# Retention with its tiles in three pools, sums of squares for two heads at a time, and two subtractions on VectorE instead of GpSimd

## The chip, the cores and the metric

The kernel runs on one NeuronCore of a Trainium2 chip. Five engines work side by side, each through its own instruction queue in order: TensorE (PE in the profile; its weight loads are listed as PEld), VectorE (DVE), ScalarE (ACT), GpSimd (POOL) and SyncE (SP). SP computes nothing; it issues nearly all of this kernel's DMAs. ACT issues the loads of the projections' weights. PE, DVE and ACT reach both on-chip memories, the large SBUF and the small PSUM into which PE writes; here POOL is used on SBUF tiles only.

The metric is the device time of one execution in microseconds (us). The kernel before took 1909.71 us, the median of three runs (1906.38, 1909.71 and 1910.21).

## What is computed

One layer of a streaming encoder on a sequence of 2048 frames with 1024 channels. A projection of the normalised input gives the operands of two branches. Branch A is chunked attention with 8 heads. Branch B, the one that matters here, is retention with 8 heads, 64 key channels and 128 value channels each. Both are gated, projected, merged, projected again, added to the input and normalised. Cut to what the change touches (`qc` is scaled, `intra_decay`, `cross_decay`, `state_decay` and `chunk_decay` are powers of the head's decay):

```python
s = einsum('bnqhd,bnkhd->bnhqk', qc, kc) * intra_decay        # scores, masked by decay
o_intra = einsum('bnhqk,bnkhe->bnqhe', s, vc)
kv = einsum('bnkhd,hk,bnkhe->nbhde', kc, state_decay, vc)
state = state * chunk_decay + kv                               # from chunk to chunk
o_cross = einsum('bnqhd,nbhde->bnqhe', qc, state_prev) * cross_decay
o = o_intra + o_cross
var = mean(square(o - mean(o)))                                # per frame and head, over 128 channels
o = (o - mean(o)) * rsqrt(var + GN_EPS) * gn_gain
```

The kernel centres the values `v` beforehand, so that the mean of `o` is zero and the variance is a plain sum of squares divided by 128.

## The kernel before

All products are made in the type fp32r, and every operand is split in two for accuracy: an upper part, which is a copy to fp32r made by ACT, and a lower part, which is the operand minus its upper part. A product is then three matmuls (upper by upper, upper by lower, lower by upper).

The program goes through these stages: projections of queries, keys and values of the first half of the sequence (`p0`), attention and retention of the first half, the same for the second half (`p1`, `heads(1)`), then the two output projections of the branches (`ba`, `br`) and the last one (`out`). The gate projections (`g0`, `g1`) have no stage of their own. They are a stream of dense matmul steps, and attention and retention call `fill(n)` to put n steps of this stream between their own matmuls. A step of the gate stream is a group of three matmuls of 512 columns. `later(n, fn)` puts work on the other engines n steps after the present one, and `put(n, dst, src)` does so for a store that SP issues. The order in which each engine gets its instructions is fixed by these calls: `keep_in_program_order` holds for all engines up to the last stages.

Retention (`retention`, L1612) treats two heads at a time (pair `p`, 0 to 3) and a stretch `st` of 256 frames. A pair and a stretch are called a unit here: 16 units in each half, 32 in all; a unit has two items, one for each head `i`. What a unit does:

- SP loads keys and queries for the scores (`load_scored`: tile `ks`, shown as kr, and two tiles `q`, shown as qr, each with two DMAs), and keys and values for the state and the output (`load_valued`: kd and two tiles vr). Each of these six tiles is 128 x 512. Keys and queries are asked for two units ahead, the others one unit ahead. Decay masks (dm, 128 x 384) are loaded once for four units of a pair.
- `scores` (L1668): four matmuls into PSUM tile sr. One step later DVE multiplies by the mask into `sm`, two steps later ACT copies the upper part `sh`, two steps later POOL subtracts into the lower part `sl` (L1692).
- `update` (L1697): the product of keys and values, and the state on DVE.
- `output` (L1742): two matmuls with the state (shown as `o<-qr,sstk`) and six with the parts of the scores. Both heads of a unit write into one PSUM bank, `o`, of which there is one.
- `evacuate` (L1759): once both heads are done, ACT copies `o` to `oz`, squares it to `o2`, and two steps later copies the squares' upper part `o2h`; two further steps later POOL makes the lower part `o2l` (L1783). SP stores `oz` (shown as `ors<-oz`). In the next unit, `sums` adds the squares up over the channels: a matmul with a one-hot column puts each sum into one row of PSUM tile `ssq`. Row `8 * b + 2 * p + i` holds 512 frames of one head, so a unit takes four matmuls of 256 columns, for two heads and two parts.

At the end of a half, `ssq` (32 rows of 512) goes through an inverse square root on DVE to DRAM (`rsscr`). `finish_yr` (L1237) later reads one head's row of 512 into all 128 partitions (tile rb) and scales by it.

All tiles of retention but the state come from one ring, `E` (L114, tag `"e"`), of `E_RET = 22` buffers of 128 x 512 fp32. A new tile takes a buffer whose tile has had its last use, and the instruction that writes it waits until that use is over: the last reader of an operand, or the landing of a store. PSUM accumulators of the gate stream come from a ring of four (`ACC`), and their sums in SBUF from a ring of six (`C`).

Of the kernel before, what the change touches and what calls it, by code (L numbers as in the profile page):

```python
# [11 lines left out]
F32 = mybir.dt.float32  # L12
F32R = mybir.dt.float32r
# [3 lines left out]
ALU = mybir.AluOpType  # L17
# [4 lines left out]
P = 128  # L22
# [6 lines left out]
B = 512  # L29
NB = SEQ // B  # L30
T = 256
# [22 lines left out]
CS = 6  # L54
E_PROJ = 19
E_ATT = 11
E_RET = 22
E_MRG = 23
PR_BUFS = 5
ATT_FILLS = (1.0, 1.0)  # L60
# [9 lines left out]
ONE = 31  # L70
# [3 lines left out]
def hybrid_kernel(  # L74
# [28 lines left out]
    epool, xpool = [None], [None]  # L103

    def r32(ap):
        return ap.bitcast(F32)
# [7 lines left out]
    def E(name, dt=F32, shape=(P, 512)):  # L114
        return epool[0].tile(list(shape), dt, tag="e", name=name)
# [4 lines left out]
    def D(name, shape, dt=F32):  # L120
        return dram.tile(list(shape), dt, name=name)

    def open_phase(name, e_bufs, tr_bufs=0):
        st = ExitStack()
        phase[0] = st
        epool[0] = st.enter_context(tc.tile_pool(name=f"e_{name}", bufs=e_bufs, reuse_waits="tile"))
        if tr_bufs:
            xpool[0] = st.enter_context(
                tc.tile_pool(name=f"tr_{name}", bufs=tr_bufs, space=PSUM, reuse_waits="tile")
            )  # L130
        return st
# [21 lines left out]
    pe, act, dve, pool = Ordered(nc.tensor), Sometimes(nc.scalar), Sometimes(nc.vector), Sometimes(nc.gpsimd)  # L153
    dma = Ordered(nc.sync).dma_start
# [9 lines left out]
    ohr = const.tile([P, NOH], F32R, name="ohr")  # L164
# [28 lines left out]
    rsscr = [D(f"rss_{s}", [32, B]) for s in range(2)]  # L193
# [51 lines left out]
    def later(n, fn):  # L245

        order[0] += 1
        deferred.append((steps[0] + n, order[0], fn, free[0]))
        deferred.sort(key=lambda e: e[:2])
# [8 lines left out]
    def put(lag, dst, src):  # L258

        later(lag, lambda: dma(dst, src))  # L260
# [75 lines left out]
    class Strassen(Chunk):  # L336
        tag = ""
# [899 lines left out]
    def finish_yr(h, b, m, lead, hold=0):  # L1237

        a, u, r = (E(f"{n}_{h}_{b}") for n in ("yr", "yv", "rb"))
        dma(a, orscr[h // 2][b][h % 2])  # L1240
        dma(u, urscr[h][b])
        dma(r, rsscr[b // 2][8 * b + h].rearrange("(o d) -> o d", o=1).broadcast_to([P, B]))

        def gated():
            dve.scalar_tensor_tensor(a, a, gn[:, h:h + 1], u, ALU.mult, ALU.mult)

        later(lead, gated)
        later(lead + 2, lambda: (pool if m is None else dve).tensor_tensor(a, a, r, ALU.mult))
        if m is None:
            put(lead + 8, yrscr[h], a)  # L1250
            return
        wh, wl = (w[:, h % 4, :] for w in R[m])
        at = max(lead + 5, hold - steps[0])
        later(at, lambda: act.copy(wh, a))
        later(at + 2, lambda: dve.tensor_tensor(wl, a, r32(wh), ALU.subtract))
# [356 lines left out]
    def retention(s, ps_ret):  # L1612
        RET_FILL = RET_FILLS[s]
        ssq = ps_ret.tile([32, 512], F32, tag="ssq", bufs=1, name="ssq")
# [3 lines left out]
        tiles, values, dms = {}, {}, {}  # L1618
        begun = [False]
# [36 lines left out]
        def load_state(p, st):  # L1656

            if st == 4:
# [2 lines left out]
                dma(r32(sstk).rearrange("p i c -> p (i c)"), r32(skscr[p]))  # L1661
                sstks[p, 4] = sstk

        def load_mask(p, i):
            dms.setdefault(p, []).append(E(f"dm_{p}_{i}")[:, 0:T + P])
            dma(dms[p][i], dmask[2 * p + i])

        def scores(p, st, i):  # L1668

            nm = f"{p}_{st}_{i}"  # L1670
            ks, qs = tiles[p, st]
            sp = ps_ret.tile([P, 512], F32, tag="sr", bufs=2, name=f"sr_{nm}")[:, 0:T + P]
            for kk in range(2):
                o = sp[:, kk * T:T + kk * P]
                kcol = ks[:, i, kk * P:(kk + 1) * P]
                pe.matmul(o, kcol, qs[i][:, 0, kk * P:], start=True, stop=False)
                pe.matmul(o, kcol, qs[i][:, 1, kk * P:], start=False, stop=True)
            got = []

            def masked():  # L1680
                sm = E(f"sm_{nm}")[:, 0:T + P]
                dve.tensor_tensor(sm, sp, dms[p][i], ALU.mult)
                later(2, lambda: high(sm))

            def high(sm):
                got.append(E(f"sh_{nm}", F32R)[:, 0:T + P])
                act.copy(got[0], sm)
                later(2, lambda: low(sm))

            def low(sm):  # L1690
                got.append(E(f"sl_{nm}", F32R)[:, 0:T + P])
                pool.tensor_tensor(got[1], sm, r32(got[0]), ALU.subtract)  # L1692

            later(1, masked)
            return got
# [41 lines left out]
        def sure(here):  # L1737

            while not here():
                emit()  # L1740
# [18 lines left out]
        def evacuate(p, st, ops):  # L1759
            b, un = st // 2, st % 2  # L1760
            nm = f"{p}_{st}"
            got = []

            def out_():
                oz = E(f"oz_{nm}")
                o2 = E(f"o2_{nm}")
                act.copy(oz, ops)
                act.activation(o2, ops, AF.Square)
                put(
                    2,  # L1770
                    orscr[p][b][:, :, un * T:(un + 1) * T].rearrange("i p t -> p i t"),
                    oz.rearrange("p (i t) -> p i t", i=2),
                )
                later(2, lambda: high(o2))

            def high(o2):
                got.append(E(f"o2h_{nm}", F32R))
                act.copy(got[0], o2)
                later(2, lambda: low(o2))

            def low(o2):
                got.append(E(f"o2l_{nm}", F32R))
                pool.tensor_tensor(got[1], o2, r32(got[0]), ALU.subtract)  # L1783

            later(1, out_)

            def sums():
                sure(lambda: len(got) == 2)
                for i in range(2):
                    r = 8 * b + 2 * p + i  # L1790
                    for n, t in enumerate(got):
                        pe.matmul(
                            ssq[:, un * T:(un + 1) * T], ohr[:, ONE - r:ONE - r + 32],
                            t[:, i * T:(i + 1) * T],
                            start=not begun[0], stop=(p == 3 and st == 4 * s + 3 and i == 1 and n == 1),
                            skip_group_check=True,
                        )
                        begun[0] = True

            return sums  # L1800

        load_scored(*todo[0])
        for i in range(2):
            load_mask(0, i)
# [53 lines left out]
    st = open_phase("proj0", E_PROJ, 4)  # L1858
# [71 lines left out]
    def heads(s):  # L1930

        st = open_phase(f"att{s}", E_ATT)
        with tc.tile_pool(name=f"sbp{s}", bufs=1, reuse_waits="tile") as sbp:
            with tc.tile_pool(name=f"ps_wide{s}", bufs=1, space=PSUM, reuse_waits="tile") as ps_wide:
                attention(s, sbp, ps_wide)
                flush()
        st.close()
        st = open_phase(f"ret{s}", E_RET)
        with tc.tile_pool(name=f"ps_ret{s}", bufs=1, space=PSUM, reuse_waits="tile") as ps_ret:
            retention(s, ps_ret)  # L1940
            flush()
        return st
# [5 lines left out]
    st = heads(0)  # L1948
# [4 lines left out]
    st = open_phase("proj1", E_PROJ, 4)  # L1953
    ch = jobs[2].chunks[1]
    ch.b = {}
    for key in ("b11", "b12", "b21", "b22"):
        ch.b[key] = E(f"{key}_p1", shape=(P, 4, P))
        j, h = int(key[1]) - 1, int(key[2]) - 1
        dma(ch.b[key], w_cols(w_in, jobs[2].cols[1], 2, j)[:, :, h * P:(h + 1) * P])
    run_to(end["g0"])  # L1960
    for h in range(HEADS):
        later(10 + 44 * h, lambda h=h: finish_yr(h, 0, None, 18))
# [4 lines left out]
    st = heads(1)  # L1967
# [4 lines left out]
    st = open_phase("mrg", E_MRG, 4)  # L1972

    free_at = end["br0"] - 12
    for s, (first, every, of) in enumerate((YR_0, YR_1)):
        for n, (i, h) in enumerate((i, h) for i in range(1 - s, 2) for h in range(HEADS)):
            hold = free_at + h % 4 if s and i and h > 3 else 0
            later(
                first + every * n // of,
                lambda s=s, i=i, h=h, hold=hold: finish_yr(h, 2 * s + i, RYR[s][i, h // 4], 8, hold),  # L1980
            )
# [60 lines left out]
```

## Time and profile before

| what | before |
|---|---|
| median of three runs | 1909.71 us |
| profiled execution | 1909.69 us |
| its span in the profile | 1907.9 us |
| mean granted TensorE clock | 0.997 of full speed |
| PE busy | 1866.9 us (98%), 10213 matmuls |
| DVE busy | 1355.7 us (71%) |
| ACT busy | 933.1 us (49%) |
| POOL busy | 665.3 us (35%) |
| retention's masked scores (`sm`), first and last start | 572.2 and 1479.1 us |

Retention takes two stretches of the span, from about 571 to 735 us and from about 1325 to 1497 us. The span is the time from the first to the last instruction of the program in the profile. Busy time is the time in which an engine has an instruction under way; matmuls overlap one another, so a busy PE may still do less than it could. In the views of groups, waits and time below, `sh<-sm` reads "the instruction that writes sh and reads sm". Nearly all instructions carry line 143, since a helper records them, so they are told apart by the tiles. A wait is put down to what came last by the semaphores.

### The profile page before, as it was taken

The page shows a single profiled execution, that of the slowest core. Times are in us where ns is not written, and L with a number is a line of the kernel's source. Part 1 is how long each engine was busy: PE and PEld are TensorE (multiplying, and loading weights), DVE is VectorE, ACT ScalarE, POOL GpSimd, SP SyncE. Part 2 cuts the span into 40 slices and gives each one's busy share as a digit, 9 for nine tenths or more (in the row PEclk, how much of TensorE's full clock was granted, in tenths as well). Part 3 has the DMA queues.
Part 4 walks back from the last instruction along what each step waited for, and adds up shares of the span by engine and source line. Part 5 has one row for each costly group of instructions (what it writes and reads, how often), then busy time and mean ns, then how long its engine had stood idle before and what let it go on. Part 6 is the DMA issues. An engine that isn't in the chain of part 4 may idle for free. (4 is left out here: it accounts for less than half of the span.)

```text
span 1907.9 us, 31062 instructions
## 1 busy us (share of the span) xinstructions
PE 1866.9 (98%) x10213; PEld 1604.4 (84%) x10213; DVE 1355.7 (71%) x2456; ACT 933.1 (49%) x1931; POOL 665.3 (35%) x583
## 2 busy tenths in 40 slices
PE   7999999999999999999999999999999999999998
PEld 6899889888888888899889888887888878888886
DVE  6879888677655658889798677765546766767665
ACT  7555554666654455443333666664455321223544
POOL 0102105455645561001105554554564000002775
PEclk9999999999999999999999999999999999999999
DMA  6586976666549987775776656555998999986673
GB/s 197 158 275 200 282 265 213 185 193 185 175 144 278 279 257 258 231 233 195 222 247 202 185 165 180 166 150 155 275 283 265 326 355 345 322 291 227 209 238 127
DMA packets 325553, 435.88 MB, mean 228 GB/s; under 512 B 29880, under 2 KB 191184, under 8 KB 325392
## 3 DMA queue, kind: packets, MB, share of 16 engines
q1 hardware_dynamic: 260096, 368.35, 60.7%
q10 hardware_dynamic: 65296, 65.55, 11.2%
q8 instruction: 81, 1.33, 0.3%
q14 instruction: 80, 0.66, 0.1%
HBM read 288.14 MB, written 145.64 MB: 227 GB/s over the span
## 5 line engine op out<-in xcount | busy, mean ns | idle before, releaser
L143 POOL TENSOR_SCALAR pr<-pr,rsum 128x640 f32<-128x640 f32 (+4 forms) x128 | 100.0, 781 | 197.7 <-DVE rsum L143 130.7
L143 DVE TENSOR_TENSOR ptl<-tp,pth 128x512 fp32r<-128x512 f32 (+1 forms) x168 | 100.3, 597 | 91.7 <-ACT pth L143 77.8
L143 ACT ACTIVATE pr<-pr,mn 128x640 f32<-128x640 f32 (+4 forms) x128 | 97.9, 765 | 123.3 <-DVE mn L143 97.3
L143 PE MATMUL ps_g_x<-r,wh_g 128*128 128x512 f32 x448 | 141.5, 397 | 1.0 <-ACT u_g L143 0.9
L143 PE MATMUL ps_g_z<-r,wh_g 128*128 128x512 f32 x448 | 141.1, 396 | 0.0
L143 POOL TENSOR_TENSOR l_vr<-vrt,h_vr 128x512 fp32r<-128x512 f32 x32 | 47.7, 1492 | 202.4 <-DMA qrs<-l_q 131.6
L143 POOL TENSOR_TENSOR t_out<-raw_out 128x512 f32<-128x512 f32 x7 | 14.1, 2008 | 263.2 <-DVE wl_out L143 263.2
L143 DVE CUSTOM_DVE_ANT_0 pr<-wide,bt 128x640 f32<-128x640 f32 (+4 forms) x128 | 93.7, 732 | 16.5 <-PE wide L143 13.5
L143 ACT CAST pth<-tp 128x512 fp32r<-128x512 f32 (+1 forms) x168 | 85.3, 507 | 38.9 <-PE tp L143 34.2
L143 PE MATMUL wide<-ka,qa 128*128 128x384 f32 (+1 forms) x448 | 94.9, 327 | 2.9 <-DVE mn L143 2.7
L143 DVE TENSOR_TENSOR sm<-sr,dm 128x384 f32<-128x384 f32 x64 | 35.6, 556 | 85.3 <-PE sr L143 33.9
L143 ACT CAST wh_p<-raw_p 128x512 fp32r<-128x512 f32 x111 | 67.9, 618 | 51.0 <-PE ps_p_y L143 18.2
L143 POOL TENSOR_TENSOR sl<-sm,sh 128x384 fp32r<-128x384 f32 x64 | 69.8, 1090 | 64.8 <-ACT sh L143 44.0
L143 PEld LDWEIGHTS tp<-ident,pr 128*128 128x128 f32 x560 | 71.8, 141 | 23.5 <-POOL pr L143 1.0
L143 PEld LDWEIGHTS ps_g_x<-r,wh_g 128*128 128x128 f32 x448 | 79.6, 189 | 13.9 <-ACT u_g L143 2.3
L143 PEld LDWEIGHTS ps_g_z<-r,wh_g 128*128 128x128 f32 x448 | 79.5, 188 | 12.4
L143 PE MATMUL tp<-ident,pr 128*128 128x128 f32 x560 | 89.0, 272 | 0.3
L143 PE MATMUL ps_g_z<-r,wl_g 128*128 128x512 f32 x224 | 88.2, 394 | 0.0
L143 PE MATMUL ps_g_x<-r,wl_g 128*128 128x512 f32 x224 | 88.1, 393 | 0.0
L143 POOL TENSOR_TENSOR wl_g<-t_g,wh_g 128x512 fp32r<-128x512 f32 x56 | 75.5, 1349 | 35.1 <-ACT wh_g L143 33.8
L143 DVE TENSOR_TENSOR wl_p<-raw_p,wh_p 128x512 fp32r<-128x512 f32 x111 | 79.5, 723 | 7.7 <-ACT wh_p L143 5.4
L143 POOL TENSOR_TENSOR t_g<-raw_g,t_g 128x512 f32<-128x512 f32 x56 | 73.8, 1318 | 28.1 <-issue 8.9
(927 smaller groups left out, 6016.7 us busy)
## 6 DMA issues: line engine op xcount, KB each, us to landing
raw_g<-in_w_in_dram ACTq DMA_DIRECT2D x56, 512.0 KB, 4.9
raw_p<-in_w_in_dram ACTq DMA_DIRECT2D x50, 512.0 KB, 5.8
qa<-qas SPq DMA_DIRECT2D x128, 128.0 KB, 3.4
qr<-qrs SPq DMA_DIRECT2D x128, 128.0 KB, 4.8
vr<-vrs SPq DMA_DIRECT2D x64, 256.0 KB, 5.6
ka<-kas SPq DMA_DIRECT2D x56, 256.0 KB, 4.1
va<-vas SPq DMA_DIRECT2D x40, 256.0 KB, 3.4
kds<-kdt_k SPq DMA_DIRECT2D x32, 256.0 KB, 4.8
```

Of the source, the lines that this page charges most:

```text
L143: return tc.keep_in_program_order(op(*a, **k))
```

## The change

There are four edits.

1. Retention's tiles come from three rings. Loads keep `E`, now with 11 buffers of 128 x 512. Masks and the three tiles of the scores (`sm`, `sh`, `sl`) come from `D_`, 9 buffers of 128 x 384. The four tiles of the output (`oz`, `o2`, `o2h`, `o2l`) come from `O_`, 4 buffers of 128 x 512. In bytes for each partition this is 22,528 + 13,824 + 8,192 = 44,544, where 22 buffers took 45,056.
2. The lower parts `sl` and `o2l` are subtracted on DVE and no longer on POOL.
3. `sums` takes both heads in one matmul of 512 columns: two matmuls for each unit and no longer four. The layout of `ssq` changes with it: row `4 * st + p` holds both heads of a unit, 256 frames each.
4. `finish_yr` reads a head's factors from two rows of this layout, 256 numbers from each, where it read 512 from one.

```diff
-E_RET = 22
+E_RET = 11
+D_RET = 9
+O_RET = 4
...
-        dma(r, rsscr[b // 2][8 * b + h].rearrange("(o d) -> o d", o=1).broadcast_to([P, B]))
+        by_head = rsscr[b // 2].rearrange("(b u p) (i t) -> b p i u t", u=2, p=4, i=2)
+        dma(
+            r.rearrange("p (u t) -> p u t", u=2),
+            by_head[b, h // 2, h % 2].rearrange("(o u) t -> o u t", o=1).broadcast_to([P, 2, T]),
+        )
...
+        def D_(name, dt=F32):
+            return epool[0].tile([P, T + P], dt, tag="d", bufs=D_RET, name=name)
+
+        def O_(name, dt=F32):
+            return epool[0].tile([P, 512], dt, tag="o", bufs=O_RET, name=name)
...
-            dms.setdefault(p, []).append(E(f"dm_{p}_{i}")[:, 0:T + P])
+            dms.setdefault(p, []).append(D_(f"dm_{p}_{i}"))
...
-                sm = E(f"sm_{nm}")[:, 0:T + P]
+                sm = D_(f"sm_{nm}")
...
-                got.append(E(f"sh_{nm}", F32R)[:, 0:T + P])
+                got.append(D_(f"sh_{nm}", F32R))
...
-                got.append(E(f"sl_{nm}", F32R)[:, 0:T + P])
-                pool.tensor_tensor(got[1], sm, r32(got[0]), ALU.subtract)
+                got.append(D_(f"sl_{nm}", F32R))
+                dve.tensor_tensor(got[1], sm, r32(got[0]), ALU.subtract)
...
-                oz = E(f"oz_{nm}")
-                o2 = E(f"o2_{nm}")
+                oz = O_(f"oz_{nm}")
+                o2 = O_(f"o2_{nm}")
...
-                got.append(E(f"o2h_{nm}", F32R))
+                got.append(O_(f"o2h_{nm}", F32R))
...
-                got.append(E(f"o2l_{nm}", F32R))
-                pool.tensor_tensor(got[1], o2, r32(got[0]), ALU.subtract)
+                got.append(O_(f"o2l_{nm}", F32R))
+                dve.tensor_tensor(got[1], o2, r32(got[0]), ALU.subtract)
...
-                for i in range(2):
-                    r = 8 * b + 2 * p + i
-                    for n, t in enumerate(got):
-                        pe.matmul(
-                            ssq[:, un * T:(un + 1) * T], ohr[:, ONE - r:ONE - r + 32],
-                            t[:, i * T:(i + 1) * T],
-                            start=not begun[0], stop=(p == 3 and st == 4 * s + 3 and i == 1 and n == 1),
-                            skip_group_check=True,
-                        )
-                        begun[0] = True
+                r = 4 * st + p
+                for n, t in enumerate(got):
+                    pe.matmul(
+                        ssq, ohr[:, ONE - r:ONE - r + 32], t, start=not begun[0],
+                        stop=(p == 3 and st == 4 * s + 3 and n == 1), skip_group_check=True,
+                    )
+                    begun[0] = True
```

## The prediction, made before the change was run

> **What bounds the kernel now.** I read the busy times first, then a table of stretches: both stretches of retention (571:735 and 1325:1497), one of projection, one of output projection, one with a dip of the clock, one of attention. The columns are busy time and instructions of PE, PEld, DVE, ACT and POOL, the granted clock, the DMA share and GB/s.
>
> ```profile
> span 1907.9 us, 31062 instructions
> PE 1866.9 (98%) x10213; PEld 1604.4 (84%) x10213; DVE 1355.7 (71%) x2456; ACT 933.1 (49%) x1931; POOL 665.3 (35%) x583
> ...
> 571.00:735.00 164.00, 156.80 (x911) 134.79 (x911) 92.54 (x179) 79.25 (x156) 93.09 (x77) 0.99 0.87 257
> 1325.00:1497.00 172.00, 168.40 (x973) 145.14 (x973) 91.33 (x173) 85.58 (x166) 91.58 (x75) 1.00 0.93 280
> 825.00:850.00 25.00, 25.00 (x211) 25.00 (x210) 21.11 (x43) 10.46 (x25) 1.30 (x1) 1.00 0.85 286
> 1575.00:1600.00 25.00, 25.00 (x112) 20.71 (x111) 15.01 (x24) 4.25 (x7) 0.00 (x0) 1.00 0.97 346
> 700.00:725.00 25.00, 22.75 (x128) 19.71 (x127) 12.58 (x22) 9.84 (x21) 14.75 (x13) 0.93 0.55 169
> 1075.00:1100.00 25.00, 24.75 (x144) 21.27 (x143) 16.76 (x39) 16.10 (x37) 15.11 (x15) 1.00 0.55 167
> ```
>
> PE sets the pace: outside retention it has no gap that this change could close. Inside, it is idle for 164.00 - 156.80 = 7.2 us and 172.00 - 168.40 = 3.6 us. This 10.8 us, and what a slower clock costs (0.93 in 700:725), is nearly all that can be won. Who holds PE there is in the waits of PE, first of the first stretch, then of the second (total, times, longest):
>
> ```profile
> PE o L143 <- ACT o L143: 4.2, 4, 2.3
> PE sr L143 <- DMA qr<-qrs: 1.0, 2, 0.6
> PE kv L143 <- DMA vr<-vrs: 0.7, 1, 0.7
> ...
> PE ssq L143 <- POOL o2l L143: 0.5, 1, 0.5
> ```
>
> ```profile
> PE o L143 <- DMA sstk<-sks: 1.4, 1, 1.4
> PE o L143 <- ACT o L143: 1.4, 1, 1.4
> PE o L143 <- POOL sl L143: 0.4, 1, 0.4
> PE ssq L143 <- POOL o2l L143: 0.2, 1, 0.2
> ```
>
> The largest, 4.2 + 1.4 = 5.6 us, is PE waiting for ACT to read the bank `o`. Why ACT is late stands in the group of `sh` and in ACT's timeline; the last row is PE's timeline at the longest of these waits.
>
> ```profile
> L143 ACT CAST sh<-sm 128x384 fp32r<-128x384 f32 x64 | 32.9, 514 | 71.8 <-DMA ors<-oz 49.9 <-DVE sm L143 18.9 <-POOL sl L143 2.2
> ```
>
> ```profile
> 667.88 0.52 ACT L143 CAST sh<-sm 128x384 fp32r<-128x384 f32 x1 [5.57 <-DMA ors<-oz]
> ...
> 669.34 0.57 ACT L143 COPY oz<-o 128x512 f32<-128x512 f32 x1
> 669.82 0.60 ACT L143 ACTIVATE o<-o 128x512 f32<-128x512 f32 x1
> ```
>
> ```profile
> 708.67 0.80 PE L143 MATMUL o<-qr,sstk 128*128 128x256 f32 x2 [2.25 <-ACT o L143]
> ```
>
> `sh` reads nothing of `oz`. It waits because it was given the buffer out of which the store of an earlier `oz` is still being read: 49.9 us in all. ACT is in order, so `oz` and the squaring queue behind `sh`, and PE behind them.
>
> **The change, part by part.** *Three rings, the ACT wait.* `sh` can no longer get a buffer of `oz`. What can be late next is `oz` itself: its ring holds just one unit's four tiles.
>
> ```profile
> 601.89 0.59 ACT L143 COPY oz<-o 128x512 f32<-128x512 f32 x1 [0.92 <-PE o L143]
> ...
> 605.45 0.40 PE L143 MATMUL o<-qr,sstk 128*128 128x256 f32 x2
> ...
> 606.66 0.39 SPq L143 DMA_DIRECT2D ors<-oz  x1
> ```
>
> ```profile
> DMA to landing us min/median/max: 2.3/5.2/7.7
> ```
>
> The second fence is from the view of the tile ors. A store is issued 606.66 - 601.89 = 4.8 us after the copy and lands 5.2 us (median) to 7.7 us (longest) later: 10.0 to 12.5 us. A unit lasts 164.00 / 16 = 10.2 us. So the next `oz` finds its buffer free half of the time and waits 2.3 us at worst. PE needs the bank 605.45 - 601.89 = 3.6 us after the start of the copy; copy and square take 669.82 + 0.60 - 669.34 = 1.1 us. The slack of 2.5 us just covers the worst wait. Of the 5.6 us between nothing and all is won; I take 4.6 and leave 1.0 for other work of ACT in the way.
>
> *The clock.* The dip in 700:725 follows the wait of 2.25 us. It costs (1 - 0.93) x 25 = 1.75 us and goes with that wait: bounds 0 and 1.75, I take 1.7.
>
> The Trainium skill, page "TensorE: Matmul & The Clock Gate", section "What's actually happening", says that the clock halves after an idle window of about 3.4 us. By that rule a gap of 2.25 us need not be punished at all; this trace shows the dip behind a shorter gap, and I go by the trace.
>
> *Three rings, the loads.* Eleven buffers hold six loads of a unit. Counted in program order, when the second query tile is asked for two units ahead, this unit's second query tile, its values and the next unit's six loads hold nine, the new keys and first query tile make eleven; the twelfth waits for the second `output` to begin.
>
> ```profile
> 598.25 3.06 SPq L143 DMA_DIRECT2D qr<-qrs  x4
> ...
> 600.82 0.40 PE L143 MATMUL o<-qr,sstk 128*128 128x256 f32 x2
> ...
> 603.78 0.34 SPq L143 DMA_DIRECT2D dm<-in_dmask_dram  x1
> ...
> 611.93 0.62 PE L143 MATMUL sr<-qr,kr 128*128 128x256 f32 x4
> ```
>
> ```profile
> DMA to landing us min/median/max: 2.6/4.8/7.2
> ```
>
> The last two of four query DMAs go out at 599.8 now and could at 601.2 then, 1.4 us later. They would be issued by 602.7, before the next entry of SP (603.78), and land by 602.7 + 7.2 = 609.9 at the latest (the view of the tile qr), ahead of their scores at 611.93. Keys, values and the first query tile need buffers freed before their turn; no `sh` or `oz` holds one any more. Bounds: the present waits for loads go (1.0 + 0.7 gained), or they triple (3.4 lost). I take a loss of 0.5.
>
> *Subtractions on DVE.* The rows that price them: the two groups that leave POOL, a DVE group of the same width that reads PSUM, a DVE group from the view of u_g with one operand in PSUM, and the subtraction of the state's lower part, both of whose operands lie in SBUF, from the view of its tile and as a group of the first stretch.
>
> ```profile
> L143 POOL TENSOR_TENSOR sl<-sm,sh 128x384 fp32r<-128x384 f32 x64 | 69.8, 1090 | 64.8 <-ACT sh L143 44.0 <-DMA raw_g<-in_w_in_dram 4.9 <-DMA qr<-qrs 3.5
> L143 POOL TENSOR_TENSOR o2l<-o,o2h 128x512 fp32r<-128x512 f32 x32 | 42.9, 1341 | 60.3 <-ACT o2h L143 24.5 <-PE o L143 15.6 <-DMA kd<-kds 4.8
> L143 DVE TENSOR_TENSOR sm<-sr,dm 128x384 f32<-128x384 f32 x64 | 35.6, 556 | 85.3 <-PE sr L143 33.9 <-DMA dm<-in_dmask_dram 18.9 <-issue 9.1
> ...
> L143 DVE TENSOR_TENSOR u_g<-ps_g_y,u_g x28: 671/692/693, 323.5 to 1455.1; 128x512 f32<-128x512 f32 x28
> ...
> L143 DVE TENSOR_TENSOR sstk<-state,sstk x28: 418/422/1397, 581.3 to 1477.4; 64x256 fp32r<-64x256 f32 x28
> ...
> L143 DVE TENSOR_TENSOR sstk<-state,sstk 64x256 fp32r<-64x256 f32 x16 | 11.8, 739 | 2.1 <-ACT sstk L143 1.6
> ```
>
> With a PSUM operand DVE's time hardly varies (671 to 693 ns). With both operands in SBUF it is stretched from 418 up to 1397 ns, about one POOL instruction more, 739 - 418 = 321 ns in the mean while POOL is busy (93.09 + 91.58) / 336 = 55%. Without 69.8 + 42.9 = 112.7 us POOL falls to 21%, so I take 321 x 21 / 55 = 0.12 us each: 64 x (0.556 + 0.12) + 32 x (0.692 + 0.12) = 69 us, with 58 and 88 as bounds (no stretch, all of it). DVE goes from 184 of 336 us (55%) to 253 (75%). PE is what hides this: DVE may lag as long as no PSUM bank or operand is late. Attention, with DVE at 16.76 / 25 = 67%, loses 0.25 of 25 us on PE; 1% of 336 would be 3.4 us. Bounds 0 and 3.4, I take a loss of 1.6. The waits of PE for POOL (0.5 + 0.2 + 0.4 = 1.1 us) go: gain 1.1, bound 0.
>
> *Sums.* 32 x 4 matmuls of 256 columns go and 32 x 2 of 512 come. Back to back they cost 25.00 / 211 = 0.1185 us (825:850) and 25.00 / 112 = 0.2232 us (1575:1600): 15.2 against 14.3 us, a gain of 0.9. Half as many instructions do the same columns.
>
> *The factors' load.* Twice as many pieces half as long, 32 times. Its waiters are few:
>
> ```profile
>   DVE yr L1248: 1.8, 3
> ```
>
> PE is full in 1575:1600 while this goes on. I take 0; without that cover it would be 1.8 us once more.
>
> *Sum:* 4.6 + 1.7 + 1.1 + 0.9 - 1.6 - 0.5 = 6.2 us. The profiled execution took 1909.69 us, 1.8 more than its span, and is as long as the median of 1909.71. Forecast: 1903.5 us.
>
> **Rivals.** *Higher gain.* All 10.8 us of idle time go, and the dip, at no loss: 1909.7 - 12.5 = 1897.2. Against it: loads at a DMA share of 0.87 to 0.93.
>
> *The wait only changes its owner.* `oz` waits for its own store, since its ring has no spare buffer, and ACT is as late as before. Of 5.6 and 1.7 us nothing is won; 0.9 + 1.1 - 1.6 - 0.5 stays: 1909.8. For it: stores landing after 12.5 us; against: the slack of 2.5 us. Halfway there lies 1906.5.
>
> *Slower: DVE takes over POOL's waits.* POOL now stands idle, at no cost to anyone, until ACT has delivered:
>
> ```profile
> POOL sl L143 <- ACT sh L143: 44.0, 20, 5.2
> POOL o2l L143 <- ACT o2h L143: 24.5, 11, 5.4
> ```
>
> On DVE, in order, the state's additions and the draining of the gates' banks queue behind such a wait, and PE waits for both. If the 68.5 us come along, DVE is taken for 253 + 68.5 of 336 us, 96%. It decides once a wait outlasts the bank's slack; if half of the 31 waits cost PE 1 us each and nothing is won at ACT, that is 15.5 - 0.9 - 1.1 + 0.5 = 14 us: 1924. With half of ACT's gain kept it is 1920. Against it: much of that wait stems from `sh` held up by the store, which goes.
>
> The Trainium skill, page "SBUF — State Buffer", section "Who interferes with whom", states that a DVE instruction with two SBUF inputs and a GpSimd instruction that reads SBUF exclude each other for the whole instruction. The stretched row agrees; the rule belongs to this rival, as it makes each moved subtraction one more that can be held.
>
> **Chances.** Forecast 0.52 (its own range 1900 to 1906), higher gain 0.14, owner changes 0.20, slower 0.14. A measurement of this kernel tells about 0.2% from no change, 3.8 us, so faster means under 1905.9. Faster: 0.48 + 0.14 + 0.01 = 0.63. Same: 0.04 + 0.19 + 0.01 = 0.24. Slower: 0.13. The range is 1897 to 1913: it leaves out most of the slower case and little else.
>
> **What would show it.** ACT's `sh` no longer waits for `ors<-oz`; `oz` does, for under 2.5 us each time. PE's wait for ACT at `o` falls from 5.6 to about 1 us, and the clock is 1.00 after 700 us. POOL's busy time falls by about 113 us, DVE's rises by 58 to 88, matmuls are 64 fewer. The forecast is wrong if PE comes to wait for DVE (banks of the gates, `sl`, `o2l`) or for qr and vr by more than 5 us in all, or if the waits at `oz` exceed 3 us.

## The result, and the profile after

| | before | after |
|---|---|---|
| median, same chip | 1910.20 us (9 runs) | 1919.88 us (9 runs) |
| lowest to highest | 1905.54 to 1911.75 us | 1911.23 to 1924.29 us |
| profiled execution | 1909.69 us | 1917.13 us |

The ratio is 1.0053, with a 95% interval of 1.0040 to 1.0065: the change makes the kernel slower by about 10 us. The prediction said 1903.5 us, 6 us faster.

The busy times after, from the first part of the page:

```profile
span 1915.3 us, 30730 instructions
...
PE 1868.8 (98%) x10149; PEld 1599.9 (84%) x10149; DVE 1416.3 (74%) x2552; ACT 934.8 (49%) x1931; POOL 562.1 (29%) x487
```

The work moved as the diff says: 64 matmuls fewer, POOL 103 us less, DVE 61 us more. The table of stretches after, with two rows for the clock and one for the output projection of the attention branch (`ba`, 1500:1575). The columns are the length, the busy time and instructions of PE, PEld, DVE, ACT and POOL, the granted clock, the DMA share and GB/s:

```profile
571.00:735.00 164.00, 156.75 (x876) 131.65 (x875) 125.17 (x227) 80.65 (x156) 40.73 (x29) 0.99 0.87 255
1325.00:1497.00 172.00, 168.09 (x937) 142.02 (x936) 121.34 (x223) 85.69 (x165) 38.18 (x27) 1.00 0.92 278
1500.00:1575.00 75.00, 66.89 (x280) 52.76 (x279) 48.71 (x76) 17.07 (x29) 0.00 (x0) 0.98 0.90 307
675.00:700.00 25.00, 22.85 (x120) 18.89 (x120) 15.22 (x33) 11.70 (x23) 2.67 (x2) 0.93 0.97 282
700.00:725.00 25.00, 24.04 (x140) 20.24 (x139) 21.09 (x34) 12.20 (x24) 8.82 (x6) 1.00 0.54 177
```

The row of the same view of before that the prediction did not look at:

```profile
1500.00:1575.00 75.00, 73.68 (x320) 59.25 (x319) 54.44 (x85) 19.80 (x33) 0.00 (x0) 1.00 0.97 342
```

Two things are to be seen. In retention PE's idle time is 7.25 and 3.9 us, where it was 7.2 and 3.6: nothing was won there, and nothing lost. The dip of the clock to 0.93 has not gone, it has moved from 700:725 to 675:700. The loss lies behind retention: in 1500:1575 PE is idle for 8.1 us and was for 1.3, and the DMA engines moved 307 GB/s in place of 342. The granted clock is 0.98 there and was 1.00, which is worth another (1 - 0.98) x 75 = 1.5 us.

**Retention: one wait out, others in.** The group of `sh` after. Its wait for the store of `oz`, 49.9 us before, is gone:

```profile
L145 ACT CAST sh<-sm 128x384 fp32r<-128x384 f32 x64 | 32.9, 513 | 46.7 <-DVE sm L145 46.7
```

PE's waits in the first and then in the second stretch of retention after (total, times, longest):

```profile
PE o L145 <- DVE sl L145: 2.8, 2, 2.1
PE ssq L145 <- DVE o2l L145: 1.8, 2, 1.6
PE sr L145 <- DMA qr<-qrs: 1.4, 1, 1.4
...
PE kv L145 <- DMA vr<-vrs: 0.4, 1, 0.4
```

```profile
PE kv L145 <- DMA vr<-vrs: 1.9, 3, 0.8
PE ssq L145 <- DVE o2l L145: 1.2, 1, 1.2
PE o L145 <- DMA sstk<-sks: 0.5, 1, 0.5
PE sr L145 <- DMA qr<-qrs: 0.4, 1, 0.4
```

PE no longer waits for ACT at `o` (5.6 us before). In its place stand 2.8 + 1.8 + 1.2 = 5.8 us for DVE and 2.3 us for `vr` (0.7 before). The longest of the new waits, in the timelines of SP, DVE and PE (start, duration, engine, and in brackets the wait ahead of it):

```profile
681.13 3.15 SPq L145 DMA_DIRECT2D qr<-qrs  x4
...
685.42 0.59 SPq L145 DMA_DIRECT2D dm<-in_dmask_dram  x1
```

```profile
688.36 0.56 DVE L145 TENSOR_TENSOR sm<-sr,dm 128x384 f32<-128x384 f32 x1 [5.10 <-DMA dm<-in_dmask_dram]
688.84 0.55 DVE L145 TENSOR_TENSOR sl<-sm,sh 128x384 fp32r<-128x384 f32 x1
```

```profile
689.44 0.39 PE L145 MATMUL o<-sl,vr 128*128 128x256 f32 x1 [2.06 <-DVE sl L145]
```

The mask of a new pair is issued behind four loads of queries and lands late; the masked score `sm` of the next item stands at the head of DVE's queue and waits 5.1 us for it; `sl` of the item before, long ready, now stands behind it in the same queue, and PE waits for `sl`. On POOL it did not stand behind `sm`. The slow clock of 675:700 follows this wait of 2.06 us.

**Behind retention: a load that lands later.** The loads of the factors, rb, in the second half (issues with their median and longest duration, DVE's waits for them in total and times, and the time to landing), before and then after:

```profile
L143 SPq DMA_DIRECT2D rb<-rss x24: 319/380/1467, 1509.3 to 1655.1; - x24
...
  DVE yr L1248: 1.8, 3
...
DMA to landing us min/median/max: 4.7/5.7/8.4
```

```profile
L145 SPq DMA_DIRECT2D rb<-rss x24: 370/371/1022, 1507.9 to 1669.1; - x24
...
  DVE yr L1254: 18.6, 16
...
DMA to landing us min/median/max: 6.4/7.2/8.5
```

Each rb lands 1.5 us later, and DVE waits for 16 of 24 in place of 3. These loads stand on SP between others that this stage needs. SP's own waits that are put down to the landing of an rb, in 1500:1600, before and then after:

```profile
SPq L143 <- DMA rb<-rss: 2.6, 6, 0.8
```

```profile
SPq L145 <- DMA rb<-rss: 8.2, 9, 2.0
```

SP's issues of the weights raw_ba, before and then after:

```profile
1518.75 0.38 SPq L143 DMA_DIRECT2D raw_ba<-in_w_out_attn_dram  x1
...
1530.64 0.38 SPq L143 DMA_DIRECT2D raw_ba<-in_w_out_attn_dram  x1
```

```profile
1519.47 0.38 SPq L145 DMA_DIRECT2D raw_ba<-in_w_out_attn_dram  x1
...
1533.49 0.38 SPq L145 DMA_DIRECT2D raw_ba<-in_w_out_attn_dram  x1
```

Two such issues lie 11.9 us apart before and 14.0 us after. What PE makes of it is in its waits in 1500:1575, before and then after:

```profile
PE ps_ba_(0, 0)_18748 L143 <- ACT wh_ba_(0, 0)_18672 L299: 0.9, 1, 0.9
PE ps_ba_(0, 0)_18556 L143 <- ACT wh_ba_(0, 0)_18476 L299: 0.4, 1, 0.4
```

```profile
PE ps_ba_(0, 0)_18393 L145 <- ACT wh_ba_(0, 0)_18313 L301: 3.3, 1, 3.3
PE ps_ba_(0, 0)_18684 L145 <- ACT wh_ba_(0, 0)_18608 L301: 2.0, 1, 2.0
PE ps_ba_(0, 0)_18492 L145 <- ACT wh_ba_(0, 0)_18412 L301: 1.4, 1, 1.4
PE ps_ba_(0, 0)_18592 L145 <- ACT wh_ba_(0, 0)_18518 L301: 1.3, 1, 1.3
```

ACT makes wh_ba from raw_ba, so PE waits 8.0 us here where it waited 1.3. The first theory was therefore: the loss is the fourth edit, the factors' load.

Theory A below is that one; its rival B is that the loss comes from the other edits. "Extra time of PE" is worked out from the trace: the time by which matmuls start later after the one before than is usual (the median, plus 15 ns) for their number of columns. It is 2.6 us in 1500:1600 before and 11.4 us after.

### The profile page after: what moved, and what is told of

Read it like the earlier page. It is cut to its first block, busy times and chain, and to the rows that moved or that the text cites. A ratio compares the mean times of both kernels' runs of the same rounds, so it can differ in the third digit from the quotient of the medians.

```text
span 1915.3 us, 30730 instructions
## 1 busy us (share of the span) xinstructions
PE 1868.8 (98%) x10149; PEld 1599.9 (84%) x10149; DVE 1416.3 (74%) x2552; ACT 934.8 (49%) x1931; POOL 562.1 (29%) x487
## 5 line engine op out<-in xcount | busy, mean ns | idle before, releaser
L145 PE MATMUL po<-pth,va 128*128 128x512 f32 (+1 forms) x224 | 75.4, 349 | 2.2 <-DVE oa L145 2.2
L145 ACT CAST wh_g<-t_g 128x512 fp32r<-128x512 f32 x112 | 68.9, 615 | 15.8 <-POOL t_g L145 9.2
```

The source lines that it names most:

```text
L145: return tc.keep_in_program_order(op(*a, **k))
```

## The experiments

All ratios are to runs of the kernel before on the same chip, with 95% intervals. The kernels ran on several chips, so two ratios are compared through the kernel before; a difference of two is uncertain by some 0.17%.

### One edit at a time

**The load undone.** The changed kernel, its rows put back into head order by the store:

```diff
-        chain.append(lambda: dma(rsscr[s], y))
+        for b in range(2 * s, 2 * s + 2):
+            for u in range(2):
+                chain.append(lambda b=b, u=u: dma(
+                    rsscr[s][8 * b:8 * b + 8, u * T:(u + 1) * T].rearrange("(p i) t -> p i t", i=2),
+                    y[8 * b + 4 * u:8 * b + 4 * u + 4].rearrange("p (i t) -> p i t", i=2)))
...
-            by_head[b, h // 2, h % 2].rearrange("(o u) t -> o u t", o=1).broadcast_to([P, 2, T]),
+        dma(r, rsscr[b // 2][8 * b + h].rearrange("(o d) -> o d", o=1).broadcast_to([P, B]))
```

> The changed kernel, with the factors' load alone undone: the rows of ssq are put back into head order when they are stored (four small stores in each half), and each rb is read as one row of 2 KB for each partition again. Theory A (the loss is the load: 256 pieces of 1 KB in place of 128 of 2 KB, in the stretch 1500:1575 where the DMA engines are full, make the weights raw_ba land late, and PE waits for wh_ba): about 9 us below the changed kernel of the same call, some 1911, and PE's waits for ACT wh_ba back from about 8 us to about 1. Rival B (the loss comes from the other edits, through what retention leaves behind): within 2 us of the changed kernel, some 1920.

Measured: 1914.81 us, ratio 1.0041 (1.0026 to 1.0055). That is below the changed kernel's 1.0053 by some 2 us, where 9 were expected. But the edit did more than was meant. SP's timeline in this kernel:

```profile
1508.82 0.71 SPq L145 DMA_DIRECT2D rss<-rt  x1
...
1510.06 0.68 SPq L145 DMA_DIRECT2D rss<-rt  x1
1510.78 0.45 SPq L145 DMA_DIRECT2D raw_ba<-in_w_out_attn_dram  x1
```

With four stores in place of one, the order on SP came out different in this stage: raw_ba, which in the kernel before goes out 5 us ahead of the store rss (1501.1 and 1506.1 us), now stands behind two of them. ACT waits 8.3 us for it, and PE's extra time in 1500:1600 is 6.6 us although rb lands at a median of 5.6 us. So the run doesn't tell the load from the order; it is replaced below by one that leaves SP's order alone.

**The load and the sums alone.** The kernel before with the third and fourth edit.

> The kernel before with the merged sums of squares and the two-row load alone; one ring of 22 and the subtractions on GpSimd as before. Theory A: about 8 us above the kernel before (9 for the load less 0.9 for the sums), some 1918. Rival B: 0 to 1 us below the kernel before, some 1909.5.

Measured: 1915.43 us, ratio 1.0048 (1.0032 to 1.0064). Nearly the whole loss comes with these two edits, in one ring and with POOL's subtractions. DVE's waits for rb are 18.8 us here too, and PE's extra time in 1500:1600 is 8.1 us.

**The subtractions back on GpSimd**, all else changed:

```diff
-                dve.tensor_tensor(got[1], sm, r32(got[0]), ALU.subtract)
+                pool.tensor_tensor(got[1], sm, r32(got[0]), ALU.subtract)
-                dve.tensor_tensor(got[1], o2, r32(got[0]), ALU.subtract)
+                pool.tensor_tensor(got[1], o2, r32(got[0]), ALU.subtract)
```

> The changed kernel with sl and o2l subtracted on GpSimd again. If the new waits of PE for DVE (ssq for o2l 3.0 us, o for sl 2.8 us, and the slow clock behind one of them, about 1.8 us) come from VectorE queueing the subtractions behind a score that waits for its mask, they go: 5 to 7 us below the changed kernel of the same call, some 1914. If VectorE is not the cause, within 2 us of it.

Measured: 1918.16 us, ratio 1.0056 (1.0037 to 1.0075): a miss, as slow as the changed kernel. PE's waits for `sl` and `o2l` fell from 5.8 to 1.8 us, but 9.9 us of extra time in 1500:1600 remained, and 1.6 us more after it. With the load as it is, what retention gains is not seen at the end: the granted clock of 1500:1575 is 0.95 in this run's profile, 0.98 in that of the changed kernel.

**The rings alone**: the first edit on the kernel before.

> The kernel before with the three rings alone. The wait of ScalarE's sh for the store of oz goes and with it PE's 5.6 us at the bank o and the dip of the clock: 5 to 7 us below the kernel before, some 1904. If that wait only changes its owner, or the eleven loads' buffers cost as much, within 2 us of the kernel before.

Measured: 1904.68 us, ratio 0.9989 (0.9977 to 1.0001). The sign is as forecast, the size is a third of it, and no gain at all still lies within the interval. The group of `sh` and PE's waits in the first stretch of retention, in this kernel:

```profile
L145 ACT CAST sh<-sm 128x384 fp32r<-128x384 f32 x64 | 32.8, 513 | 36.2 <-DVE sm L145 32.8 <-DMA vr<-vrs 2.3 <-POOL sl L145 1.2
```

```profile
PE ssq L145 <- POOL o2l L145: 1.6, 2, 1.2
PE sr L145 <- DMA qr<-qrs: 1.1, 1, 1.1
PE kv L145 <- DMA vr<-vrs: 0.7, 1, 0.7
...
PE o L145 <- ACT o L145: 0.4, 1, 0.4
```

The wait at `o` is gone as forecast (4.2 to 0.4); the one for `o2l` grew from 0.5 to 1.6.

### Is it the load, or the sums?

All slow kernels so far had the merged sums, and the fast one had not. Four kernels tell them apart; all four have SP's order of before in this stage. In the three with merged sums rb is read as one row of 2 KB. These three leave out the reordering that the new layout needs, so they scale by other rows' factors; their times alone are used. The split alone, on the kernel before, rows in DRAM kept but each cut into two pieces with a gap:

```diff
-    rsscr = [D(f"rss_{s}", [32, B]) for s in range(2)]
+    rsscr = [D(f"rss_{s}", [32, 2, 320]) for s in range(2)]
...
-        dma(r, rsscr[b // 2][8 * b + h].rearrange("(o d) -> o d", o=1).broadcast_to([P, B]))
+        dma(r.rearrange("p (u t) -> p u t", u=2),
+            rsscr[b // 2][8 * b + h, :, 0:T].rearrange("(o u) t -> o u t", o=1).broadcast_to([P, 2, T]))
```

> The kernel before, with one thing changed: each row of the factors lies in DRAM as two pieces of 256 numbers with a gap of 64 between them, so that each rb is read as 256 pieces of 1 KB and no longer as 128 of 2 KB. Rings, subtractions, sums and the values are those of before. Theory A (the split load is the loss): rb lands about 2 us later each time in 1500:1575, the loads behind it on SP drift, PE waits there go from 2.6 to about 8 us, and the time is 5 to 8 us above the kernel before, some 1914. Rival C (the merged sums are the loss, since every slow kernel so far has them): within 1 us of the kernel before.

> The kernel before with the merged sums of squares alone; each rb is read as one row of 2 KB as before. (With the new layout of ssq that row holds the wrong factors: only the time counts here.) Theory A: 0 to 1 us below the kernel before. Rival C: 5 to 8 us above it.

> Three rings and the merged sums, subtractions on GpSimd, rb as one row of 2 KB (which holds the wrong factors: only the time counts). Theory A: what the rings alone gave, less at most 1 us: 2 to 4 us below the kernel before, some 1904. Rival C: 4 to 6 us above the kernel before.

> The changed kernel with rb read as one row of 2 KB, and the store of the factors as in the changed kernel, so that the order of SP's queue is that of before (the row holds the wrong factors: only the time counts). It differs from the run with rings and sums by the subtractions on VectorE alone. If VectorE costs what the waits of PE in retention show (ssq for o2l 3.0 us, o for sl 2.8 us, clock 1.8 us): 4 to 8 us above that run, some 1910, and no loss in 1500:1575. If it costs nothing: within 1.5 us of that run.

| kernel | median us | ratio |
|---|---|---|
| split alone, pieces 1.25 KB apart | 1907.19 | 1.0006 (0.9990 to 1.0022) |
| sums alone | 1906.89 | 1.0004 (0.9990 to 1.0019) |
| rings and sums | 1907.26 | 1.0002 (0.9990 to 1.0014) |
| the changed kernel, rb as one row | 1909.24 | 1.0009 (0.9995 to 1.0024) |

Both theories fall. Neither the sums nor pieces of 1 KB cost anything that shows: rb as 256 of them lands at a median of 5.5 us. Yet the changed kernel without its two-row read loses only 0.09%, so the loss is in that read. What distinguishes it from the harmless split is where the pieces lie: row `8b + p` and row `8b + 4 + p`, four rows of 2 KB, which is 8 KB apart.

### The distance of the two pieces

```diff
-    rsscr = [D(f"rss_{s}", [32, 2, 320]) for s in range(2)]      # split alone: 1.25 KB apart
+    rsscr = [D(f"rss_{s}", [32, 2, 2048]) for s in range(2)]     # 8 KB; 1024 for 4 KB, 4096 for 16 KB
```

```diff
-    rsscr = [D(f"rss_{s}", [32, B]) for s in range(2)]           # the changed kernel: 8 KB apart
+    rsscr = [D(f"rss_{s}", [32, B + 64]) for s in range(2)]      # padded rows: 9 KB apart
```

```diff
-                r = 4 * st + p                                   # the changed kernel
+                r = 8 * b + 2 * p + un                           # neighbouring rows: 2 KB apart
```

> The kernel before with rb read as 256 pieces of 1 KB, as in the run with the split alone, but with the two pieces of a row 8 KB apart, as the rows of the changed kernel are (there they were 1.25 KB apart, and cost nothing). Theory D (the distance of the two pieces is the loss: reads that go to and fro between two places 8 KB apart are stretched): rb lands at a median of about 7 us and not 5.5, PE waits in 1500:1575 rise from 2.6 to about 8 us, and the time is 6 to 9 us above the kernel before. Rival E (the loss needs the merged sums and the split together): within 1.5 us of the kernel before.

> The changed kernel with the rows of the factors in DRAM padded from 512 to 576 numbers, so that the two pieces of an rb lie 9 KB and not 8 KB apart. If it is 8 KB as such (the same place of the memory's banks), the loss goes: 6 to 9 us below the changed kernel, some 1911, with rb landing at a median of 5.5 to 6 us. If any far distance costs, it stays at some 1918.

> The changed kernel with the rows of ssq in another order (8b + 2p + u in place of 8b + 4u + p), so that the two rows of an rb are neighbours, 2 KB apart. Theory D: rb lands at 5.5 to 6 us, PE waits in 1500:1575 fall from 11.4 to about 3 us, and the time is 6 to 9 us below the changed kernel: within 3 us of the kernel before. Rival E: some 1918, as the changed kernel.

> The same with sl and o2l subtracted on GpSimd again: all of the change but the move to VectorE, with the load mended. If the move costs what PE's new waits for VectorE in retention show, 3 to 5 us below the run with neighbouring rows; and 0 to 4 us below the kernel before. If it costs nothing, within 1.5 us of the run with neighbouring rows.

> The kernel before with rb read as two pieces of 1 KB for each partition that lie 4 KB apart. If the loss is one of powers of two from 4 KB up: 8 to 16 us above the kernel before, as at 8 KB. If it begins at 8 KB: within 2 us of the kernel before, as at 1.25 KB.

> The kernel before with rb read as two pieces of 1 KB for each partition that lie 16 KB apart. If the distance costs by being a multiple of 8 KB: 8 to 16 us above the kernel before. If 8 KB is a place of its own: within 3 us of the kernel before.

The loads of rb in the second half, for pieces 8 KB apart and then 4 KB apart, both on the kernel before (DVE's waits for them, and the time to landing):

```profile
  DVE yr L1251: 22.5, 16
...
DMA to landing us min/median/max: 6.5/7.6/9.5
```

```profile
  DVE yr L1251: 2.0, 2
DMA to landing us min/median/max: 4.6/6.0/8.3
```

The same numbers for all of them, with the ratios:

| rb | on | landing, median us | DVE's waits for rb, us (times) | ratio |
|---|---|---|---|---|
| one piece of 2 KB | before | 5.7 | 1.8 (3) | 1 |
| two, 1.25 KB apart | before | 5.5 | 2.3 (2) | 1.0006 (0.9990 to 1.0022) |
| two, 4 KB apart | before | 6.0 | 2.0 (2) | 0.9998 (0.9986 to 1.0011) |
| two, 8 KB apart | before | 7.6 | 22.5 (16) | 1.0074 (1.0060 to 1.0087) |
| two, 16 KB apart | before | 7.5 | 22.3 (18) | 1.0087 (1.0074 to 1.0100) |
| two, 8 KB apart | changed | 7.2 | 18.6 (16) | 1.0053 (1.0040 to 1.0065) |
| two, 9 KB apart | changed | 6.4 | 5.1 (4) | 1.0019 (1.0008 to 1.0030) |
| two, 2 KB apart | changed | 5.9 | 1.1 (1) | 1.0012 (1.0000 to 1.0024) |

Theory D holds, from both sides. The kernel before with the split load is as fast as without it at 1.25 and 4 KB, and slower by 0.74% at 8 KB; the changed kernel, with nothing changed but the order of 32 rows, gets 0.53 - 0.12 = 0.41% back, some 8 us. The changed kernel with rb as one row gave about the same (1.0009). It is not distance as such: 16 KB costs, and of the 8 us at 8 KB little is left at 9 KB.

On the kernel before, the loss at 8 KB is 14 us, where 6 to 9 were expected, and nearly twice that of the changed kernel. Part of this shows in the profiles: PE's extra time goes on in 1600:1700 (6.6 us at 8 KB, 7.3 at 16 KB, none in the changed kernel), and the granted clock of 1500:1575 is 0.95 at 8 KB, and 0.98 at 16 KB and in the changed kernel. Why the loss goes on behind 1600 us stays open.

Counted among the 1 KB packets that started in 1500:1660 on the kernel before, those over 100 ns are 349 of 13,677 at 1.25 KB, 330 of 13,718 at 4 KB, 1035 of 12,047 at 8 KB and 1331 of 11,840 at 16 KB, while the median is 46 ns for all. Some packets are stretched, not all. Why places 8 and 16 KB apart do this to a load in which 128 partitions read the same two pieces was not tried further; that the memory's banks are behind it, as one expectation supposed, no run shows.

The Trainium skill, page "DMA: Bandwidth & Descriptors", section "Latency and other measured facts", tells of a loss at row pitches of large powers of two, from 512 KiB up, and infers that streams in lock step meet in the same channel; padding by 4 KiB cured it there and by 192 bytes did not. Here the pitch is 8 KB, the pattern another, and 1 KB of padding takes most of the loss away (1.0053 to 1.0019).

The run with neighbouring rows and GpSimd came out at 0.9998 (0.9987 to 1.0009), against 1.0012 with VectorE: the move costs some 0.14%, about 2.7 us, a little less than the 3 to 5 us expected. The pair of kernels with rb as one row (1.0009 against 1.0002) says 0.07%. In both pairs the intervals overlap, so a price of the move on the time is likely but not shown.

### Masks earlier

```diff
-            if n % 8 in (4, 6) and p < 3:
-                load_mask(p + 1, n % 8 // 2 - 2)
+            if n % 8 in (2, 4) and p < 3:
+                load_mask(p + 1, n % 8 // 2 - 1)
```

> The changed kernel with neighbouring rows, and the masks of the next pair asked for one unit earlier (items 2 and 4 of a pair in place of 4 and 6). Theory (VectorE's queue stands behind a score that waits for its mask): sm's wait for the mask goes from about 20 us to under 3, PE's waits for sl and o2l from 4.4 us to about 1, and the time is 2 to 4 us below the run with neighbouring rows. Rival (VectorE is simply slower at it, or held by GpSimd): those waits stay, and the time is within 1 us.

> The same with the subtractions on GpSimd. Theory: GpSimd has let VectorE's late scores pass already, so early masks bring less here: 0 to 2 us below the run with neighbouring rows and GpSimd. Rival: 2 to 4 us, the same as on VectorE, since the late score itself is what PE waits for.

> The kernel before with the three rings and early masks; subtractions on GpSimd, sums and load as before. If merged sums and neighbouring rows add nothing to the time, this is as fast as the run with early masks and GpSimd: 0.2% below the kernel before, some 1903. If the sums of 512 columns were the gain, within 1.5 us of the kernel before.

> The kernel before with early masks alone, in the one ring of 22. If late masks are the larger stall and the rings bring little of their own: 2 to 4 us below the kernel before. If the wait of sh for the store of oz stays the bound in one ring: within 1.5 us of the kernel before, and PE's wait for ScalarE at o stays at 2 to 6 us.

| kernel with early masks | median us | ratio | the same with late masks |
|---|---|---|---|
| changed, neighbouring rows | 1903.91 | 0.9984 (0.9975 to 0.9993) | 1.0012 |
| that, with GpSimd | 1901.96 | 0.9980 (0.9968 to 0.9992) | 0.9998 |
| rings alone | 1903.82 | 0.9973 (0.9958 to 0.9987) | 0.9989 |
| before, one ring | 1915.25 | 1.0041 (1.0027 to 1.0054) | 1 |

The group of `sm` with neighbouring rows and VectorE, late masks and then early ones:

```profile
L145 DVE TENSOR_TENSOR sm<-sr,dm 128x384 f32<-128x384 f32 x64 | 35.5, 554 | 38.3 <-DMA dm<-in_dmask_dram 27.8 <-PE sr L145 5.5 <-PE ps_g_y L145 4.4
```

```profile
L145 DVE TENSOR_TENSOR sm<-sr,dm 128x384 f32<-128x384 f32 x64 | 35.4, 554 | 21.9 <-PE sr L145 16.1 <-PE ps_g_y L145 4.6 <-DMA qr<-qrs 0.5
```

The wait for the mask went from 27.8 us to none, and PE's waits for `sl` and `o2l` from 2.4 + 1.4 + 0.6 = 4.4 us to 0.8 + 1.4 = 2.2. The time fell by 0.28%, 5 us, more than the theory's 2 to 4. The kernel with GpSimd gained too, 0.18%, so a late score cost something there as well. With the masks early the two engines lie 0.04% apart, within both intervals. That fits a late mask as what made VectorE's queue expensive: the waits show it, while in time the two engines differ by less than the noise with late masks and with early ones.

The last row was not expected. In one ring early masks make the kernel slower. Its `sm` shows why in part:

```profile
L143 DVE TENSOR_TENSOR sm<-sr,dm 128x384 f32<-128x384 f32 x64 | 35.5, 555 | 85.0 <-PE sr L143 32.9 <-DMA ors<-oz 16.1 <-issue 8.4
```

A mask asked for earlier takes another turn in the ring, and now `sm` as well gets buffers that a store still reads (16.1 us; before, it is not among the three largest waits of `sm`); PE's waits for ACT at `o` stay at 3.2 + 3.1 = 6.3 us. The profiled execution, 1911.10 us, is the fastest of its eight, so the rest of the 0.41% cannot be read from it and stays open. With early masks the rings are worth 1.0041 - 0.9973 = 0.68%, some 13 us; with late ones 0.11%.

Three of these kernels beat both the kernel before and the changed one. The lowest ratio is that of rings and early masks alone; the lowest median that of all edits but the move to VectorE, with neighbouring rows and early masks. The data don't tell them apart.

## Why the prediction was wrong, by its own steps

**The factors' load, taken at 0: the step that failed.** The prediction counted "twice as many pieces half as long" and priced them at 0, or 1.8 us without cover. The count did not matter (1.0006). What it did not weigh is the new layout's address: two pieces 8 KB apart. That costs 0.41%, about 8 us, of the 10 us lost. The cover failed as well. "PE is full in 1575:1600 while this goes on" is true after too, but the loads begin at 1508, and in 1500:1575 the weights raw_ba stand on the same queue behind them. DVE, the waiter that was looked at, waits 18.6 us, but the loss reaches PE by SP's queue: SP waits 8.2 us for these landings in place of 2.6, the weights behind them go out later, and PE waits 8.0 us for what ACT makes of them.

**Subtractions on DVE, forecast a loss of 1.6 and a gain of 1.1 us.** The groups after:

```profile
L145 DVE TENSOR_TENSOR sl<-sm,sh 128x384 fp32r<-128x384 f32 x64 | 54.5, 852 | 4.1 <-ACT sh L145 3.5
...
L145 DVE TENSOR_TENSOR o2l<-o,o2h 128x512 fp32r<-128x512 f32 x32 | 24.1, 753 | 0.6 <-ACT o2h L145 0.6
```

54.5 + 24.1 = 78.6 us where 69 was taken and 58 to 88 was the bound: size about right. The share taken for the stretch was not: `sl` took 0.30 us more than `sm`, where 0.12 was taken, though POOL was busy for only (40.73 + 38.18) / 336 = 23% of the time. The price in time came out at 1.3 to 2.7 us, neither clear of noise, where a net 0.5 was taken. The rival "DVE takes over POOL's waits" named the right mechanism (an instruction in order behind a waiting one, PE waiting for both) but the wrong waiter: DVE waits for ACT at `sl` only 3.5 us in all. It is `sl` that stands behind `sm`, which waits 20.9 us for masks:

```profile
DVE sm L145 <- DMA dm<-in_dmask_dram: 20.9, 6, 5.1
```

The prediction's own fence showed that wait in the group of `sm` before (18.9 us), and did not ask what would be queued behind it. PE's 5.8 us for `sl` and `o2l` pass the 5 us at which the prediction called itself wrong.

**Three rings, forecast +4.6, +1.7 for the clock and -0.5.** The mechanism was right: `sh` no longer waits, `oz` waits for its store 4.1 us in all, 2.2 us at most, and the squaring behind it 5.0 us for the same stores. With rings alone one wait of `oz` is 3.9 us, above the 3 us at which the prediction called itself wrong. The group of `oz` after:

```profile
L145 ACT COPY oz<-o 128x512 f32<-128x512 f32 x32 | 18.7, 585 | 28.5 <-PE o L145 24.3 <-DMA ors<-oz 4.1
```

The size was not: 0.11% alone, 2 us with an interval from a gain of 4.4 us to none. One reason is the base. PE's wait for ACT at `o` is 5.6 us in the one execution that was read, and 5.4, 4.3, 3.4, 2.8, 2.5 and 2.2 us in the profiles of the six other kernels with one ring and late masks (split alone, 16 KB apart, 4 KB apart, sums alone, 8 KB apart, sums and load): a mean of 3.7, of which 0 to 0.4 remain with rings. The other is what came late next: PE's wait for `o2l` went from 0.7 to 1.6 us. With rings and GpSimd (rings alone, rings and sums, GpSimd again, neighbouring rows with GpSimd) the granted clock is 1.00 in both stretches of retention, as the term for the clock had it (with one ring and late masks it is so in one profile of seven); after the change a dip stands behind the new wait for `sl`. Not every such wait brings one: with padded rows PE waited 2.43 us for sstk in 1325:1497, and the granted clock there is 1.00.

**Sums, forecast +0.9.** Alone 1.0004 (0.9990 to 1.0019): neither shown nor excluded.

**The whole, in parts**, by the differences of the ratios: 0.53% lost = 0.41% for the distance of the pieces + 0.14% for VectorE behind late masks - 0.02% for the rest (rings, sums, and the load in two near pieces). The first part is uncertain by 0.17%, the second by 0.16%, the third by 0.11%, so only the first is clear of noise. Against the forecast this is 8 us at the load, where 0 was taken, about 6 us at rings and sums, where 4.6 + 1.7 - 0.5 + 0.9 = 6.7 us were to be won and 0.4 were, and about 2 us at the subtractions.

## What to carry to other kernels

When a layout in DRAM changes, look not only at how many pieces a load has but at how far apart they lie: 8 or 16 KB between the two pieces made this load land 1.5 to 2 us later, and another order of rows cured it at no cost. Before work is moved to an engine, list the instructions on it that wait for transfers, since all that is moved stands behind them; mending the late transfer may be worth more than the move. A stall that appears in one execution is a draw: read it in several before it is priced.

## What the runs showed that had not been expected

- Reading two 1 KB pieces for each of 128 partitions costs nothing that shows beside one piece of 2 KB when they lie 1.25, 2 or 4 KB apart, and 14 to 17 us of this kernel when they lie 8 or 16 KB apart (ratios 1.0074 and 1.0087); at 9 KB, on the changed kernel, most of its loss is gone (1.0019 against 1.0053).
- The granted clock fell to 0.93 in the mean of a 25 us slice behind a wait of PE of 2.06 us, as before behind one of 2.25 us, and did not behind one of 2.43 us with padded rows. The Trainium skill, page "TensorE: Matmul & The Clock Gate", section "What's actually happening", gives an idle window of about 3.4 us; all three gaps here are shorter.
- On DVE `sl`, with both operands in SBUF, took 852 ns in the mean and 552 in the median, up to 1668, as the stretched row in the prediction let one expect.
- Asking for a transfer earlier made the kernel with one shared ring slower (1.0041) and the kernel with separate rings faster (0.9973).
